# Attention values as the fixed operand of the value product, probabilities of two row blocks as the moving one

## The chip, the cores and the metric

The kernel runs on one core of a Trainium2 chip. The metric is the device time of one execution in microseconds; the median of three runs stands for a kernel. The engines are TensorE (PE, with its weight loads as PEld), VectorE (DVE), ScalarE (ACT), GpSimd (POOL) and SyncE (SP), which mostly starts transfers.

## The reference, cut to what matters

One step of a hybrid encoder layer on 1040 prompt rows (16 learned ones and 1024) and 32 sample rows with a cache of 512. Four mixers of 256 columns each; two of them are attention with 4 heads of 64. The prompt rows attend causally to the prompt rows.

```python
def fox_attend(q, k, v, f_q, f_k, q_pos, k_pos):          # mixer B, key "f" in the kernel
    s = jnp.einsum('bqhd,bkhd->bhqk', q, k).astype(jnp.float32) * (HEAD_DIM ** -0.5)
    s = s + (jnp.moveaxis(f_q, 2, 1)[..., :, None] - jnp.moveaxis(f_k, 2, 1)[..., None, :])
    s = jnp.where(k_pos[None, :] <= q_pos[:, None], s, -jnp.inf)
    p = jax.nn.softmax(s, axis=-1)
    return jnp.einsum('bhqk,bkhd->bqhd', p, v.astype(jnp.float32))

def sb_attend(q, k, v, q_pos, k_pos):                     # mixer C, key "s"
    z = jnp.einsum('bqhd,bkhd->bhqk', q, k).astype(jnp.float32) * (HEAD_DIM ** -0.5)
    mask = k_pos[None, :] < q_pos[:, None]
    log_keep = jnp.where(mask, jax.nn.log_sigmoid(-z), 0.0)
    later = lax.cumsum(log_keep, axis=3, reverse=True) - log_keep
    w = jnp.where(mask, jnp.exp(jax.nn.log_sigmoid(z) + later), 0.0)
    return jnp.einsum('bhqk,bkhd->bqhd', w, v.astype(jnp.float32))
...
    cat = jnp.concatenate([rms_norm(out_a, gains[0]), rms_norm(out_b..., gains[1]),
                           rms_norm(out_c..., gains[2]), o_d...], axis=-1)
    out = cat @ P['w_o'][l]
```

## The kernel before, in words

All products that matter for precision run in rounded parts: an operand x is written as hi (x rounded to fp32r) and lo (x - hi, rounded), and a product is hi*hi + lo*hi + hi*lo. ScalarE writes hi, GpSimd or VectorE writes lo. The exceptions are products in plain f32, the value product of attention among them.

The program is one long sequence: input norm and projections, the recurrent mixers, then `attention` (about 495 to 860 us of the span), then the FFN. Rows of the sequence are cut into 9 blocks `TB`: block 0 has 48 rows (32 sample rows, 16 learned ones), blocks 1 to 8 have 128. `attention` runs over key "s" (stick-breaking), then "f" (forgetting); in each over 4 heads, in each over the row blocks in the order `ROWS`, of which block 8 is cut into two chunks of keys: 10 positions a head, 40 a half. At each position t a software pipeline issues stage 0 of position t, stage 1 of t-1 and so on, in the order `ORDER`; `None` in it issues products of other work from the generators `fill` (projections of mixer f, output projections `w_o` of mixers a, d, s). That sets the priority of instructions; a planner of the framework orders them by priority as their operands and buffers come free.

Stages for "s": 0 scores on PE into two banks and a ScalarE copy; 1 `softplus_log`: min(z, 40) on VectorE, exp and ln on ScalarE; 2 `sb_sums`: max on VectorE, a running sum on VectorE, z minus the sum on GpSimd; 3 exp on ScalarE. For "f": 0 scores, bias and row maximum on VectorE; 1 exp on ScalarE. Then, for both, stage 4 `attn_turn`: PE transposes each 128x128 block of probabilities with the identity; VectorE copies the turned first 16 keys (L1338), VectorE or ScalarE copy the banks of four blocks to a tile `pt` (L1349, L142). Stage 5 `attn_row`: per row block one product per key block, the turned probabilities as the fixed operand, V (128 keys x 64 columns, for "f" 65 with a column of ones) as the moving one:

```python
self.mm(o, t0[:, :n], vm[:, h, :], True, j == 0)
for kb in range(1, j + 1):
    self.mm(o, pt[:, kb - 1, :], vt[(kb - 1) // 4][:, (kb - 1) % 4, h, :], False, kb == j)
```

The result has rows on partitions. VectorE writes it to `ot` (L1369), for "f" divided by the sum in column 64 (L1366, L176). `cat_rows` later turns `ot` on PE (L187) and copies it with the norm's gain to `cx` on ScalarE, splits it and multiplies with `w_o`; the rms comes from a ScalarE square with a row sum.

V comes from `proj_t_units`, which stores it to DRAM row by row; `load_v` reads it back in pieces of 64 columns. Score tiles are in slots of tag E, V and stacked queries and keys in slots U and T; `SLOTS` gives the numbers for U, E and X. `sample_attn` treats the 32 sample rows of all heads at once.

## Time and profile before

| | |
|---|---|
| median of 3 runs | 1669.48 us (1665.16 to 1672.03) |
| profiled execution | 1677.21 us, span 1675.5 us |
| mean granted clock of TensorE | 0.962 of full speed |
| PE busy | 1543.9 us (92%), 10536 instructions |
| PE weight loads | 1364.2 us (81%) |
| VectorE busy | 986.6 us (59%), 2008 |
| ScalarE busy | 681.3 us (41%), 1295 |
| GpSimd busy | 878.8 us (52%), 819 |

Shares of the whole span are averages over stages with different limits; the rows below are taken from the two halves of `attention`. In names of groups `out<-in1,in2` the first operand of a PE instruction is the moving one, the second the fixed one. A PE instruction's duration is a latency: neighbours overlap, and what one costs is the distance between starts.

### The profile page before, as it was taken

The page shows a single profiled execution, that of the slowest core. Times are in us where ns is not written, and L with a number is a line of the kernel's source. Part 1 is how long each engine was busy: PE and PEld are TensorE (multiplying, and loading weights), DVE is VectorE, ACT ScalarE, POOL GpSimd, SP SyncE. Part 2 cuts the span into 40 slices and gives each one's busy share as a digit, 9 for nine tenths or more (in the row PEclk, how much of TensorE's full clock was granted, in tenths as well). Part 3 has the DMA queues.
Part 4 walks back from the last instruction along what each step waited for, and adds up shares of the span by engine and source line. Part 5 has one row for each costly group of instructions (what it writes and reads, how often), then busy time and mean ns, then how long its engine had stood idle before and what let it go on. Part 6 is the DMA issues. An engine that isn't in the chain of part 4 may idle for free.

```text
span 1675.5 us, 27752 instructions
## 1 busy us (share of the span) xinstructions
PE 1543.9 (92%) x10536; PEld 1364.2 (81%) x10536; DVE 986.6 (59%) x2008; ACT 681.3 (41%) x1295; POOL 878.8 (52%) x819
## 2 busy tenths in 40 slices
PE   6988997799998999999987899999999999999997
PEld 4978986787778777778866899999999998878775
DVE  9835559844436688765687744444444443455466
ACT  4535424232234455544475333333333344333241
POOL 4563233342334335321028866776777769767575
PEclk9989999999999999999997899999999999999999
DMA  5152111312363742332030222222222247535460
GB/s 158 52 172 69 40 54 53 96 47 59 98 175 106 190 114 57 88 77 65 1 129 13 64 77 77 77 77 77 78 77 74 74 148 258 206 133 201 145 212 29
DMA packets 125934, 167.36 MB, mean 100 GB/s; under 512 B 23562, under 2 KB 102388, under 8 KB 125800
## 3 DMA queue, kind: packets, MB, share of 16 engines
q1 hardware_dynamic: 110969, 138.06, 26.8%
q10 hardware_dynamic: 14735, 27.51, 4.9%
q8 instruction: 83, 1.36, 0.4%
q14 instruction: 51, 0.42, 0.1%
q0 software_dynamic: 96, 0.01, 0.0%
HBM read 121.69 MB, written 43.86 MB: 99 GB/s over the span
## 4 chain that ended last, share of the span: by engine, by line
PE 38%; DVE 9%; POOL 6%; issue 4%; ACT 2%; DMA 1%; DVEq 0%; POOLq 0%; SPq 0%; ACTq 0%
PE ps L1877 14%; PE ps L183 11%; PE mm L183 6%; PE mm L1877 5%; DVE fy L180 3%; POOL wl L171 2%; PE ps L187 2%; PE pw L183 1%; POOL wlo L171 1%; POOL h L171 1%; DVE h L171 1%; DVE ws L171 1%; DMA wr<-in_ffn_w_in 1%; DVE fx L171 1%; POOL xl L171 1%
## 5 line engine op out<-in xcount | busy, mean ns | idle before, releaser
L1877 PE MATMUL ps<-xh,whi 128*128 128x256 f32 (+1 forms) x920 | 268.6, 292 | 20.4 <-DVE fu L171 11.5
L1877 PE MATMUL ps<-xl,whi 128*128 128x256 f32 (+1 forms) x920 | 266.3, 290 | 1.6 <-DVE xl L171 1.6
L1877 PE MATMUL ps<-xh,wlo 128*128 128x256 f32 (+1 forms) x920 | 266.0, 289 | 0.0
L1877 PEld LDWEIGHTS ps<-xh,whi 128*128 128x128 f32 x920 | 177.3, 193 | 24.8 <-DVE fu L171 14.0
L1877 PEld LDWEIGHTS ps<-xl,whi 128*128 128x128 f32 x920 | 177.5, 193 | 2.2 <-DVE xl L171 2.2
L1877 PEld LDWEIGHTS ps<-xh,wlo 128*128 128x128 f32 x920 | 177.2, 193 | 0.0
L171 POOL TENSOR_TENSOR wl<-wr,wh 128x1024 fp32r<-128x1024 f32 x58 | 147.4, 2551 | 31.8 <-ACT wh L142 30.5
L171 POOL TENSOR_TENSOR wlo<-ws,whi 128x512 fp32r<-128x512 f32 x92 | 127.6, 1388 | 36.1 <-ACT whi L142 27.9
L171 POOL TENSOR_TENSOR wlo<-wst,whi 128x512 fp32r<-128x512 f32 x54 | 73.6, 1368 | 91.0 <-ACT whi L142 73.5
L171 POOL TENSOR_TENSOR wlo<-wr,whi 128x512 fp32r<-128x512 f32 x69 | 92.6, 1342 | 37.7 <-ACT whi L142 37.7
L142 ACT ACTIVATE wh<-wr 128x1024 fp32r<-128x1024 f32 x58 | 60.7, 1057 | 125.0 <-POOL wl L171 110.1
L171 DVE TENSOR_TENSOR al<-ax,ah 128x768 fp32r<-128x768 f32 (+1 forms) x33 | 61.7, 1869 | 79.8 <-ACT ah L142 71.2
L142 ACT ACTIVATE whi<-ws 128x512 fp32r<-128x512 f32 x92 | 57.6, 626 | 122.8 <-PE ps L1877 53.6
L183 PE MATMUL ps<-wh,ah 128*128 128x512 f32 x264 | 104.8, 397 | 1.6 <-DVE h L171 1.6
L183 PE MATMUL ps<-wl,ah 128*128 128x512 f32 x264 | 104.6, 396 | 0.0
L183 PE MATMUL ps<-wh,al 128*128 128x512 f32 x264 | 104.5, 396 | 0.0
L180 DVE SCALAR_TENSOR_TENSOR fy<-fx,cf,fy 128x546 f32<-128x546 f32 (+1 forms) x88 | 97.1, 1119 | 11.2 <-ACT fy L143 9.4
L171 POOL TENSOR_TENSOR clo<-cx,chi 128x256 fp32r<-128x256 f32 (+1 forms) x36 | 27.6, 768 | 134.3 <-ACT chi L142 100.2
L1877 PE MATMUL mm<-xl,whi 128*128 128x274 f32 (+1 forms) x312 | 90.6, 290 | 4.7 <-DVE xl L171 2.5
L1877 PE MATMUL mm<-xh,whi 128*128 128x274 f32 (+1 forms) x312 | 90.6, 290 | 2.6 <-DVE fy L171 1.9
L1877 PE MATMUL mm<-xh,wlo 128*128 128x274 f32 (+1 forms) x312 | 90.3, 290 | 0.0
L183 PE MATMUL mm<-hh,whi 128*128 128x384 f32 (+1 forms) x240 | 85.8, 358 | 1.2 <-ACT ks L1209 1.2
(514 smaller groups left out, 4495.7 us busy)
## 6 DMA issues: line engine op xcount, KB each, us to landing
wr<-in_ffn_w_out SPq DMA_DIRECT2D x58, 512.0 KB
wr<-in_ffn_w_in SPq DMA_DIRECT2D x44, 512.0 KB
actd<-fy ACTq DMA_DIRECT2D x22, 529.0 KB
wst<-in_w_in SPq DMA_DIRECT2D x44, 256.0 KB
ax<-actd SPq DMA_DIRECT2D x22, 384.0 KB
x<-in_x_prompt SPq DMA_DIRECT2D x8, 512.0 KB
hd<-x SPq DMA_DIRECT2D x8, 512.0 KB
wst<-in_w_o SPq DMA_DIRECT2D x16, 256.0 KB
```

The source lines that it names most:

```text
L142: return self.nc.scalar.activation(out, in_, f, scale=scale, **k)
L171: return (eng or self.nc.vector).tensor_tensor(out, a, b, op)
L180: return (eng or self.nc.vector).scalar_tensor_tensor(out, a, s, b, op0, op1)
L183: return self.nc.tensor.matmul(out, l, r, start=start, stop=stop)
L187: return self.nc.tensor.transpose(out, in_, self.ident[:n, :n])
L1877: self.nc.tensor.matmul(ps, l[:, k], r[:, k], start=start and k + j == 0, stop=stop and k == 3 and j == 2, skip_group_check=not start)
```

## The change

V is split into hi and lo when it is projected and stored as two interleaved parts, so that a key block of a head is a fixed operand of 128 keys by 128 columns: 64 of hi beside 64 of lo. The probabilities of two neighbouring row blocks (1 and 2 with block 0, 3 and 4, 5 and 6, 7 and 8), turned, are the moving operand with up to 256 columns (272 with block 0), once their hi part and once their lo part. ScalarE writes hi from PSUM, VectorE lo. The result has features on partitions, the product with V's hi part in one half of them and with its lo part in the other; ScalarE copies the one and VectorE adds the other. `attn_pair` is a generator: a step of it issues one bank of transposes and the products of the bank before; `ORDER` has two steps ("p") per position.

The forgetting mixer takes the row sum from the exponential's accumulator and scales the probabilities by its reciprocal in a stage of its own (`fox_scale`). `softplus_log` computes ln(1 + exp(-|z|)) and adds max(z, 0) in `sb_sums`. The outputs need no turning before `w_o`; the norm's gain goes into the weights of `w_o`, and the sum of squares over features is a product with a column of ones (`rms_rows`). `fox_past`, a part of `fox_logf`, moves to just before the sample rows of the forgetting half. Slots: E 9 instead of 8, U 10 instead of 9, no X; three buffers each for the turned hi and lo parts. The order of row blocks changes.

```diff
             if key == "g":
+                nc.scalar.dma_start(dr[tb, :n], v[:n])
                 continue
+            vh, vl = self.H("vhi", 256, F32R), self.H("vlo", 256, F32R)
+            self.act(vh[:n], v[:n], AF.Copy)
+            self.tt(vl[:n], v[:n], vh[:n].bitcast(F32), OP.subtract, nc.gpsimd)
+            for t, o, step in ((vh, 0, 192), (vl, 64, 64)):
+                nc.scalar.dma_start(AP(dr, tb * P * 512 + o, [[512, n], [256, 2], [step, 2], [1, 64]]),
+                                    t[:n].bitcast(F32).rearrange("p (a e d) -> p a e d", a=2, e=2))
+            if tb == 0:
+                nc.scalar.dma_start(self.vs[key], v[:NS])
...
@@ -1276,22 +1292,20 @@
 
     def load_v(self, key):
 
-        nc = self.nc
-        vw = 65 if key == "f" else 64
...
+        v0 = self.U("v0", F32R, 768)
+        vm, vs = v0[:, 0:512], v0[:32, 512:768].bitcast(F32).rearrange("p (h d) -> p h d", h=4)
+        self.ts(vm, self.ones[:, 0:1].to_broadcast([P, 512]), 0.0, None, OP.mult)
+        vt = [self.U("v" + key, F32R, 1024, tag).rearrange("p (b h d) -> p b h d", b=2, h=4) for _ in range(4)]
+        dr = self.vd[key]
+        nc.sync.dma_start(vs.rearrange("p h d -> p (h d)"), self.vs[key])
+        nc.sync.dma_start(vm[:NM].bitcast(F32), dr[0, 32:48])
+        for i, t in enumerate(vt):
+            nc.sync.dma_start(t.bitcast(F32).rearrange("p b h d -> p b (h d)"),
+                              dr[1 + 2 * i:3 + 2 * i].rearrange("b p c -> p b c"))
+        return vs, vm.rearrange("p (h d) -> p h d", h=4), vt
...
+    def attn_pair(self, key, h, js, rows, done):
+        nc = self.nc
+        _, vm, vt = self.V[key]
+        pr, e = divmod(h, 2)
+        ja, jb = js
+        m = NM if ja == 1 else 0
+        w = 2 * P + m
+        o = None
+        def split(hi, lo, ps):
+            self.act(hi, ps, AF.Copy)
+            self.tt(lo, ps, hi.bitcast(F32), OP.subtract)
+        ps = self.PS()
+        c = 0
+        for j in ([0] if m else []) + [ja, jb]:
+            d = rows[key, h, j]
+            self.tr(ps[:16, c:c + d["n"]], d["blocks"][0])
+            c += d["n"]
+        th, tl = self.t0
+        split(th[:16, :w], tl[:16, :w], ps[:16, :w])
+        parts = [(vm[:, h], th[:, :w], tl[:, :w], 0)]
+        yield
+        for a in range(1, jb, 2):
+            late, parts = parts, []
             ps = self.PS()
+            c = 0
+            for kb in (a, a + 1):
+                c0 = c
+                for j in js:
+                    if kb <= j:
+                        self.tr(ps[:, c:c + P], rows[key, h, j]["blocks"][kb])
+                        c += P
+                parts.append((vt[(kb - 1) // 2][:, (kb - 1) % 2, h], c0, c, w - (c - c0)))
+            hi, lo = (self.up.tile([P, 512], F32R, name=self.nm(x), tag=x, bufs=NPT) for x in ("ph", "pl"))
+            split(hi[:, :c], lo[:, :c], ps[:, :c])
+            parts = [(v, hi[:, c0:c1], lo[:, c0:c1], at) for v, c0, c1, at in parts]
+            if o is None:
+                o = self.PS()
+            for v, x, y, at in late:
+                self.mm(o[:, at:w], v, x, a == 1, False)
+                self.mm(o[:, at:w], v, y, False, False)
+            yield
+        for i, (v, x, y, at) in enumerate(parts):
+            self.mm(o[:, at:w], v, x, False, False)
+            self.mm(o[:, at:w], v, y, False, i == len(parts) - 1)
+        own, other = slice(64 * e, 64 * e + 64), slice(64 - 64 * e, 128 - 64 * e)
+        o0, ot = self.ot[key]
+        u = ot[(ja - 1) // 4]
+        at = P * ((ja - 1) % 4)
+        for dst, src in (((o0[:, pr, 32:48], slice(0, m)),) if m else ()) + ((u[:, pr, at:at + 2 * P], slice(m, w)),):
+            self.act(dst[own], o[own, src], AF.Copy)
+            self.tt(dst[own], dst[own], o[other, src], OP.add)
+        for j in ([0] if m else []) + [ja, jb]:
+            del rows[key, h, j]
+            done(j)
...
-        stages = {"f": {0: self.fox_max, 1: self.fox_exp},
+        V, st, rows = self.V, self.stacks, {}
+        stages = {"f": {0: self.fox_max, 1: self.fox_exp, 2: self.fox_scale},
                   "s": {0: self.sb_scores, 1: self.sb_log, 2: self.sb_sum, 3: self.sb_exp}}
...
+        pairs, ready = deque(), {}
+        t = 0
+        def turned(key, h, j):
+            nonlocal fill, last
+            left = ready.setdefault((key, h), set(range(9)))
+            left.discard(j)
+            if key == "s" and h == 3 and not left:
+                for _ in fill:
+                    pass
+                fill = self.w_o_units("s")
+            if (key, h) == ("f", 3):
+                if last is None:
+                    last = self.w_o_units("f")
+                late.append((t + 1, j))
+        def step():
+            while pairs and next(pairs[0], "end") == "end":
+                pairs.popleft()
+        while t < len(runs) + 5 or pairs or late:
             if t == heads[1] - EARLY_A:
                 next(fill)
             if t == half - 8:
                 self.open_mixer("f")
             if t == half + 3:
-                self.sample_attn("f", V["f"][0], ot["f"][0], self.sample_load("f"))
+                self.fox_past()
+                self.sample_attn("f", V["f"][0], self.sample_load("f"))
...
+                if s == "p":
+                    step()
+                    continue
...
                 elif c[0] == 0 and s == 4:
-                    d["turned"] = self.attn_turn(key, j, d["blocks"], d["n"])
-                elif c[0] == 0 and s == 5:
...
+                    d["ready"] = True
+                    js = (j, j + 1) if j % 2 else (j - 1, j)
+                    if j and all(rows.get((key, h, i), {}).get("ready") for i in ((0, 1, 2) if j < 3 else js)):
+                        pairs.append(self.attn_pair(key, h, js, rows, lambda i, k=key, hh=h: turned(k, hh, i)))
...
-                i = ROWS.index(j)
+                i = WROWS.index(j)
...
-        self.act(p, p, AF.Exp, bias=d["mx"][:n, 2:3])
+        self.act(p, p, AF.Exp, bias=d["mx"][:n, 2:3], accum_out=d["mx"][:n, 3:4])
+        self.nc.vector.reciprocal(d["mx"][:n, 4:5], d["mx"][:n, 3:4])
+    def fox_scale(self, d, a, b, k0, k1):
+        if a:
+            return
+        n, j = d["n"], d["j"]
+        p = d["s"][:n, 0:16 + P * j]
+        self.act(p, p, AF.Copy, scale=d["mx"][:n, 4:5])
         d["blocks"] = self.row_blocks(0, j, p)
...
-        self.ts(e, z, 40.0, None, OP.min)
-        self.act(e, e, AF.Exp)
+        self.act(e, z, AF.Abs)
+        self.act(e, e, AF.Exp, scale=-1.0)
         self.act(e, e, AF.Ln, bias=1.0)
...
-        self.tt(e, z, e, OP.max)
+        self.stt(e, z, 0.0, e, OP.max, OP.add)
...
-        kc = self.E("kc", F32, 1024).rearrange("p (b d) -> p b d", b=4)
+        tag = "T" if key == "f" else "E"
+        kc = self.U("kc", F32, 1024, tag).rearrange("p (b d) -> p b d", b=4)
         nc.sync.dma_start(kc, I[kn].rearrange("a b (n p) h d -> p (a b n) (h d)", p=P))
...
+        vc = self.U("vc", F32, 1024, tag).rearrange("p (b h d) -> p b h d", b=4, h=4)
+        nc.sync.dma_start(vc.rearrange("p b h d -> p b (h d)"), I[vn].rearrange("a b (n p) h d -> p (a b n) (h d)", p=P))
...
+        gains = self.grp_g[:, 2 * {"f": 1, "s": 2}[mixer]:][:, 0:2] if mixer in "fs" else None
+        return [load(self.I["w_o"], P * k0, 2, 512 * half, 512, gains=gains) for half in range(2)]
...
+        if mixer in "fs":
+            x = self.ot_rows(mixer, tb)
+        else:
+            x = view("cx", F32)
...
-        else:
-            i = {"f": 1, "s": 2}[mixer]
-            ps = self.PS()
-            for pr in range(2):
-                self.tr(ps[:, P * pr:P * pr + n], ot[tb][:n, P * pr:P * pr + P])
-                self.act(x[:, pr], ps[:, P * pr:P * pr + n], AF.Copy, scale=self.grp_g[:, 2 * i + pr:2 * i + pr + 1])
+        hi, lo = view("chi", F32R), view("clo", F32R)
         self.act(hi, x, AF.Copy)
         self.tt(lo, x, hi.bitcast(F32), OP.subtract, self.nc.gpsimd)
         return [[a[:, k] for k in range(2)] for a in (hi, lo)]
...
+    def rms_rows(self, mixer, tbs, v, r, tm):
+        nc = self.nc
+        ps = self.PS()
+        for tb in tbs:
+            n = TB[tb][1]
+            sq = self.S1("sq").rearrange("p (a t) -> p a t", a=2)[:, :, :n]
+            self.act(sq, self.ot_rows(mixer, tb), AF.Square)
+            self.tt(sq[:, 0], sq[:, 0], sq[:, 1], OP.add, nc.gpsimd)
+            self.mm(ps[:n, tb:tb + 1], sq[:, 0], self.ones[:, 0:1], True, True)
+        a, c = tbs[0], slice(max(tbs[0], 1), tbs[-1] + 1)
+        if a == 0:
+            self.ts(v[:48, 0:1], ps[:48, 0:1], 1.0 / 256, RMS_EPS, OP.mult, OP.add)
+        self.ts(v[:, c], ps[:, c], 1.0 / 256, RMS_EPS, OP.mult, OP.add)
+        c = slice(a, tbs[-1] + 1)
+        self.rsqrt(r[:, c], v[:, c], tm[:, c])
...
             v, r = self.rms(i)
             tm = self.C([P, 9], f"rmst{i}")
+            if mixer == "s":
+                self.rms_rows(mixer, range(9), v, r, tm)
...
-            n, c = TB[tb][1], slice(tb, tb + 1)
-            x = self.cat_rows(mixer, tb, ot)
-            if ot is not None:
-                sq = self.S1("aosq")[:n]
-                self.act(sq, ot[tb][:n], AF.Square, accum_out=v[:n, c])
-                self.ts(v[:n, c], v[:n, c], 1.0 / 256, RMS_EPS, OP.mult, OP.add)
-                self.rsqrt(r[:n, c], v[:n, c], tm[:n, c])
-            return x
-
-        nx = rows(ROWS[0])
+            if mixer == "f":
+                for tbs in ((0, 1, 2), (3, 4), (5, 6), (7, 8)):
+                    if tb == next(j for j in WROWS if j in tbs):
+                        self.rms_rows(mixer, tbs, v, r, tm)
+            return self.cat_rows(mixer, tb)
...
-LATE_C = "mneg_r selh pt0".split()
-SLOTS = 9, 8, 2
+LATE_C = "mneg_r selh o0s o0f t0h t0l".split()
+SLOTS = 10, 9, 0
+NPT = 3
...
-ORDER = 0, 1, 3, 2, None, 5, 4
+ORDER = 0, 1, 3, 2, None, "p", 4, "p"
...
-ROWS = [0, 8, 1, 7, 2, 6, 5, 3, 4]
+ROWS = [0, 8, 7, 1, 2, 6, 5, 3, 4]
+WROWS = [7, 8, 0, 1, 2, 5, 6, 3, 4]
```

## Rows read from the trace of the kernel before

**Rows 1.** Windows: us; busy us of PE, PEld, DVE, ACT, POOL; clock; DMA

```profile
495.00:716.00 221.00, 201.21 (x1278) 166.30 (x1278) 170.57 (x363) 116.25 (x255) 87.34 (x76) 0.95 0.44 114
716.00:860.00 144.00, 142.44 (x907) 115.73 (x906) 93.96 (x359) 71.08 (x174) 19.86 (x23) 0.99 0.20 53
```

**Rows 2.** Chain of waits, shares by line: 716 to 868, then 560 to 716

```profile
by line: PE ps L183 32.5%; PE mm L183 30.4%; PE ps L187 16.3%; PE pw L183 13.3%; DVE h L180 2.2%; DVE bst L1746 1.6%; DVE bmv L171 1.0%; DVE h L171 0.9%; DVE rmst L180 0.8%; issue 0.7%; DVE bmv L176 0.2%; DVE rmst L171 0.2%; DVE rmst L177 0
...
by line: PE ps L183 4.7%; DVE sbe L1491 3.3%; PE mm L183 3.0%; PE pw L183 2.4%; ACT sbe L143 2.2%; DVE sbe L171 2.2%; POOL sbe L171 2.1%; DVE sb L176 1.9%; PE ps L187 1.5%; DVE sb L1491 1.3%; DVE h L171 1.3%; DVE pt L1349 1.1%; DVE sb L171 
```

**Rows 3.** Timeline of PE: start us, us, line, output<-moving,stationary, shapes, count

```profile
760.21 0.43 PE L183 MATMUL ps<-v,pt 16*128 16x65 f32 x2
760.57 2.00 PE L183 MATMUL ps<-vf,pt 128*128 128x65 f32 x16
762.41 0.38 PE L187 MATMUL ps<-ident,s 128*16 128x128 f32 x2
...
763.00 0.22 PE L183 MATMUL pw<-mneg_r,identr 128*128 128x128 f32 x1
763.06 0.28 PE L187 MATMUL ps<-ident,ot 128*128 128x128 f32 x1
```

**Rows 4.** Timeline of PE, first and last of 21 starts

```profile
527.45 0.28 PE L183 MATMUL mm<-wlo,hh 128*128 128x256 f32 x1
...
529.82 0.28 PE L183 MATMUL mm<-whi,hl 128*128 128x256 f32 x1
```

**Rows 5.** DVE by shape, 495 to 716: busy us, mean ns, idle before

```profile
L1257 DVE TENSOR_TENSOR_SCAN nfs<-ones,nfs 4x512 f32<-4x512 f32 x1 | 1.2, 1187 | 0.0
```

**Rows 6.** Groups by shape of ACT, 495 to 716

```profile
L142 ACT ACTIVATE pt<-ps 128x512 f32<-128x512 f32 x8 | 4.7, 589 | 2.4 <-PE ps L187 2.2
...
L142 ACT ACTIVATE pt<-ps 128x256 f32<-128x256 f32 x8 | 3.0, 376 | 6.5 <-PE ps L187 6.5
...
L142 ACT ACTIVATE pt<-ps 128x384 f32<-128x384 f32 x4 | 1.9, 474 | 0.7 <-PE ps L187 0.7
```

**Rows 7.** Groups by line of ACT, 495 to 716

```profile
L143 ACT ACTIVATE sbe<-sbe 128x896 f32<-128x896 f32 (+3 forms) x48 | 41.6, 874 | 33.9 <-POOL sbe L171 28.1 <-DVE sbe L176 5.8
L143 ACT ACTIVATE sb<-sb 128x144 f32<-128x144 f32 (+4 forms) x72 | 28.0, 405 | 18.8 <-POOL sb L171 14.1 <-DVE sb L176 4.4
...
L142 ACT ACTIVATE pt<-ps 128x512 f32<-128x512 f32 (+3 forms) x24 | 10.7, 447 | 16.1 <-PE ps L187 16.0
```

**Rows 8.** Groups by line of ACT, 716 to 862

```profile
L143 ACT ACTIVATE s<-s,mx 128x912 f32<-128x912 f32 (+8 forms) x33 | 24.4, 741 | 17.4 <-DVE mx L1472 17.4
L142 ACT ACTIVATE pt<-ps 128x512 f32<-128x512 f32 (+3 forms) x32 | 16.5, 517 | 41.8 <-PE ps L187 41.7
L142 ACT ACTIVATE cx<-ps,cf 128x128 f32<-128x128 f32 (+1 forms) x34 | 12.1, 355 | 11.7 <-PE ps L187 11.4
...
L143 ACT ACTIVATION_READ_ACCUMULATOR aosq<-ot 128x1 f32 x9 | 1.8, 195 | 0.0
```

**Rows 9.** Groups by line of DVE, 495 to 716

```profile
L176 DVE TENSOR_SCALAR sb<-sb 128x144 f32<-128x144 f32 (+4 forms) x24 | 14.0, 583 | 4.9 <-ACT sb L142 4.8
L1349 DVE COPY pt<-ps 128x512 f32<-128x512 f32 (+2 forms) x24 | 13.9, 581 | 1.9 <-PE ps L187 1.9
L176 DVE TENSOR_SCALAR sbe<-sbz 128x896 f32<-128x896 f32 (+3 forms) x16 | 13.5, 846 | 1.4 <-ACT sbz L142 1.4
...
L171 DVE TENSOR_TENSOR h<-h,mm 128x512 f32<-128x512 f32 (+1 forms) x17 | 11.3, 667 | 1.4 <-PE mm L183 1.3
L1338 DVE COPY pt<-ps 16x128 f32<-16x128 f32 (+1 forms) x36 | 9.2, 255 | 3.0 <-PE ps L187 2.8
L1369 DVE COPY ot<-ps 128x64 f32<-128x64 f32 x32 | 6.8, 211 | 8.5 <-PE ps L183 8.3
```

**Rows 10.** Windows of 20 us with a lower clock, columns as in rows 1

```profile
580.00:600.00 20.00, 17.73 (x100) 14.56 (x99) 19.81 (x34) 9.76 (x19) 7.40 (x7) 0.84 0.38 102
...
880.00:900.00 20.00, 13.64 (x68) 11.78 (x69) 14.52 (x14) 11.74 (x19) 20.00 (x11) 0.67 0.00 1
```

185 lines of the change are left out of this document (65 added, 120 removed).

## Prediction

> **What bounds the kernel now.** The windows by stage come first, because the change stays inside two of them. Values are multiplied from about 495 to 860 us: the stick-breaking half to 716, the forgetting half after it. In [rows 1] the second column is TensorE's busy time. In the forgetting half it is 142.4 of 144 us at a granted clock of 0.99, with VectorE at 94 and ScalarE at 71. The chain of waits agrees: from 716 to 868 us its shares by line are nearly all PE, 32.5% at L183 into `ps` (the value products) and 16.3% at L187 (transposes) [rows 2]. That half is bound by TensorE, and time taken from PE there comes back almost whole. The stick-breaking half is mixed: PE 201, VectorE 171, ScalarE 116, GpSimd 87 of 221 us, and its chain runs through all four [rows 1, 2]. There a saving on one engine comes back in part.
>
> **What a value product costs now.** In the timeline, `x16` of the value products start at 760.57 and the next instruction at 762.41 [rows 3]: 16 records in 1.84 us, 0.115 each. Each key block is two records, so 0.230 us per block and row block. The 16-key product takes from 760.21 to 760.57, 0.36 us. A head has 36 blocks and 8 full 16-key products (row block 0 left out): 36 x 0.230 + 8 x 0.36 = 11.2 us.
>
> **What it costs afterwards.** A product in rounded parts with 256 moving columns has a row: from 527.45 to 529.82 lie 20 gaps, so 0.119 each [rows 4]; with 128 columns one starts at 763.00 and the next instruction at 763.06, 0.06 [rows 3]. Over the pairs (1,2), (3,4), (5,6), (7,8) a head has 2+4+6+8 = 20 products that serve both row blocks (the first also serves row block 0, with 272 columns) and 4 that serve one, each for the high and the low part: 40 x 0.119 + 8 x 0.06 = 5.2 us. So 6.0 us of PE go per head, 24 per half, 48 in all. The transposes of the probabilities keep their number.
>
> The Trainium skill, "FP8 and Floating Point Precision", TensorE Precision Notes, counts a true FP32 product as four passes through the array. By that an old block of 65 columns would stream 260 columns, 0.108 us by estimate at the higher clock, and the new block 2 x 128, the same: nothing would be saved on PE. The trace has two records and 0.230 us per block, so the rule is a rival with a small chance (below).
>
> **Other PE work.** Turning the outputs before the output projection goes: 36 transposes over both mixers, 128 columns and a weight load each like the records of [rows 3], 0.115 by those, so 4. The sums of squares come as 18 products with one column, two records each: 36 x 0.115 = 4 back (bounds: nothing, if they slip between, and 36 x 0.36/2 = 6.5). These cancel. But each new product waits for a ScalarE square and a GpSimd addition and stands in PE's order. For the stick-breaking mixer all nine come in a row at the change of halves: nine times a square like the 0.4 us pass in [rows 6] is 4 us of possible stall, and four groups in the forgetting half are like it, 1 us each. The cover is w_o and score products already queued; if it fails, 8 us. I take 4. `fox_past` moves from the fifth row block of the first w_o product to just before the sample rows of the forgetting half: one small SP load behind those of the cached keys and values, four transposes, three VectorE operations (a scan of 512 takes 1.2 [rows 5]) and two GpSimd selects. On PE the sample scores and all that stands behind them would wait. I take 0, since the first forgetting scores are queued ahead; uncovered it is the two scans and the minus pass, about 3, beside the load. The cached tiles move to T slots, free once the last odd head's scores are done: 0 for the same reason.
>
> **ScalarE takes over what PE and VectorE give up.** Stick-breaking: a pass for |z| comes, as large as one of the three passes in (41.6 + 28.0)/3 = 23 us [rows 7]. Splitting comes: per head 6 banks of 512 at 0.589, 4 of 384 at 0.474 and 4 first parts at the 0.376 of 256 columns [rows 6]: 6.9 us, 28 per half. The old copies (10.7) go [rows 7]. Output copies come, 4 per head at 0.376: 6. Net about +46: 116 becomes 162. Forgetting: a pass that scales the probabilities comes, as large as the exponentials (24.4 for 33, so 26 for 36 [rows 8]); reading 36 row sums, 0.19 by the sum read after the squares [rows 8], 7; splits 28; output copies 6; squares of the other mixer 4 and eight gains on weights at about 0.6, 5. The old copies (16.5) and the turned outputs (12.1) go [rows 8]. Net +47, some 5 of it hidden because neighbouring passes overlap: 71 becomes about 113.
>
> **VectorE.** Stick-breaking gives up the minimum (13.5 + 14.0), copies (13.9 + 9.2) and output copies (6.8): 57 us [rows 9]. It takes the low parts: 24 banks at the 0.667 of a pass with a PSUM operand over 512 columns, 16 of 384 (0.55, scaled from the same row), 16 small ones at 0.4: 31; output additions 7. Net -19: 171 becomes 152. The maximum that becomes a maximum and an addition keeps its size: nothing. The forgetting half gets about 10 more, beside 94: hidden.
>
> The Trainium skill, "ScalarE: Activation LUTs", Rules for kernel authors, gives minima, additions and multiplications to VectorE and not to ScalarE, against two moves of this change. Here the rows don't show VectorE ahead: 40 minima took 27.5 us [rows 9], one ScalarE pass of the same size 23 [rows 7]. By the rule VectorE would return less and ScalarE would bind sooner, which is the third case.
>
> **The sum.** Forgetting half: PE 144 - 24 + 4 = 124, above ScalarE's 113; with two engines this close I add 4 for hand-overs (a pair runs PE, ScalarE, VectorE, PE): 128, so -16. Stick-breaking half: engines at 177, 162 and 152 where they were 201, 116 and 171. If PE alone sets its length, which was 1.10 times PE's busy time, 177 gives 195, -26. If the chain through VectorE and ScalarE sets it, VectorE's -19 is half eaten by the extra ScalarE passes in the same chain, -10. No row decides between them; I take the middle, -18. The end: row blocks 3 and 4 now end together, after one more stage and up to three pair steps, so one more row's evacuation and statistics stand after the last value product: +2 (bounds 0, if the queued w_o products cover it, and 6). V is written in more, smaller pieces and read in longer ones, under the projections, with 18 extra ScalarE copies there: 0 (cover: dense PE work; without it 18 x 0.4 = 7, and -2 if the longer reads help). Together -16 - 18 + 2 = -32. The profiled execution took 1677.2 us around its span of 1675.5, 7.7 above the median of 1669.5; -32 gives 1645 against it and **1637** beside the median.
>
> **Rivals.**
> First: everything comes back. PE's 48 us, plus the waits that VectorE's 19 causes in the first half (its chain shows VectorE lines [rows 2]), -50 to -60: 1610 to 1620. For it: PE fills the forgetting half. Against it: ScalarE's 113 is only 11 behind.
> Second: ScalarE and the clock take most of it. ScalarE's queue is in order, and the splits feed PE, so each pass ahead of a split is a PE wait; and when PE waits its clock falls: 0.84 between 580 and 600 us with PE busy 17.7 of 20, 0.67 between 880 and 900 with 13.6 [rows 10]. If the first half ran at 0.84 instead of its 0.95, its 177 us of PE become 200 and nothing is left there; -16 and +2 remain, with up to 8 of stalls against them or a third of the first half's -18 kept: -6 to -20, 1650 to 1663.
> Third, slower: the buffers. A row's score tile was free after stage 4; now it lives until its pair is turned. By the order of rows and two pair steps a position, some 10 tiles (and in the forgetting half two bias tiles) want 9 E slots around position 8 of each head, so the scores of the last two row blocks wait for pair (7,8). A position is 221/40 = 5.5 us in the first half, 144/40 = 3.6 in the second; two lost positions a head are 4 x 11 + 4 x 7.2 = 73 us, and 73 - 48 + 2 = +27: 1696. It decides from a loss of 6 us a head, about one position in the first half. Against it: PE has w_o products to fill with, and the average demand fits.
> Fourth: the change doesn't do what it says: the saving on PE isn't there (four passes in the old product, or the new ones stream slower than [rows 4]): ScalarE's additions then cost what they can't hide, 1668 to 1676.
>
> **How the numbers follow.** Forecast 1637 (1625 to 1648) 0.46; first rival 0.16; second 0.24, of which 0.04 lies within 0.5%; third 0.10, most of it slower, a little of it (0.02) within; fourth 0.04, within or slower. A measurement tells about 0.5% (8 us) from no change, so faster is below 1661: 0.46 + 0.16 + 0.20 = 0.82; same 0.08; slower 0.10. The range, 1611 to 1667, leaves out the slower cases and the far end of the first.
>
> **What would show it.** Value products of 256 columns starting about 0.12 us apart, a forgetting half of about 128 us still led by PE with ScalarE near 110, a stick-breaking half near 203. Wrong if scores wait for score tiles, if PE's largest wait in either half is a ScalarE split, or if the clock in the first half falls below 0.9.

## The result, and the profile after

The kernel after takes 1692.95 us (median of 6 runs, 1680.14 to 1694.85) against 1670.46 for the kernel before (6 runs): ratio 1.0127, 95% interval 1.0084 to 1.0169. It is slower by some 22 us; forecast were 32 us less. Its profiled execution took 1694.13 us around a span of 1692.4, 16.9 more than the span before.

Where do they lie? The stages of the two programs stand at different times, so fixed windows compare different work. The cuts below are made at the same events: the first score of the stick-breaking half (PE, `pw<-kst,qst` of row block 0), of its second head, of the forgetting half, and the first FFN product. Windows of before, columns as in [rows 1]:

```profile
0.00:491.60 491.60, 434.83 (x3386) 386.31 (x3387) 295.59 (x701) 187.17 (x394) 192.58 (x246) 0.96 0.29 86
491.60:553.60 62.00, 56.45 (x420) 50.67 (x418) 37.86 (x69) 27.80 (x54) 24.87 (x19) 0.96 0.53 151
553.60:685.00 131.40, 119.96 (x678) 96.43 (x677) 110.75 (x212) 73.84 (x156) 57.14 (x51) 0.92 0.41 105
685.00:879.70 194.70, 183.66 (x1170) 148.19 (x1168) 132.97 (x498) 100.19 (x249) 32.04 (x36) 0.98 0.26 72
879.70:1675.50 795.80, 749.04 (x4889) 682.64 (x4889) 409.41 (x530) 292.31 (x445) 572.15 (x469) 0.97 0.33 110
```

The same five of after, and the two fixed windows of [rows 1] again:

```profile
0.00:497.00 497.00, 442.09 (x3378) 393.58 (x3379) 295.96 (x703) 190.88 (x404) 199.17 (x255) 0.94 0.30 89
497.00:567.60 70.60, 54.66 (x376) 48.89 (x373) 30.89 (x44) 35.53 (x73) 29.18 (x27) 0.93 0.46 128
567.60:711.50 143.90, 114.51 (x576) 89.37 (x577) 113.64 (x176) 101.48 (x222) 55.66 (x47) 0.86 0.40 111
711.50:898.10 186.60, 166.85 (x984) 136.17 (x982) 139.97 (x424) 136.08 (x310) 40.16 (x53) 0.93 0.27 78
898.10:1692.40 794.30, 749.36 (x4889) 682.84 (x4889) 409.97 (x530) 293.28 (x446) 571.49 (x470) 0.97 0.33 111
...
495.00:716.00 221.00, 171.35 (x962) 139.85 (x962) 149.27 (x226) 140.51 (x300) 86.42 (x75) 0.88 0.43 120
716.00:860.00 144.00, 136.44 (x830) 113.04 (x831) 101.41 (x293) 109.37 (x253) 29.98 (x41) 0.92 0.23 58
```

To the first score +5.4, first stick-breaking head +8.6, the three others +12.5, forgetting half -8.1, the rest -1.5. Read the third row of both: TensorE has 5 us less to do and the stage is 12.5 longer; VectorE, which was to give up work, has 3 us more; ScalarE 28 more; the granted clock fell from 0.92 to 0.86. No engine is full. The last two rows mislead: 149 for VectorE between 495 and 716 is close to the forecast's 152, but the window of before had 31 us of the forgetting half in it, that of after less than 5.

TensorE's own change is as forecast. PE's timeline of after, high and low parts with 256 columns 0.12 us apart, with 128 columns 0.06, against [rows 3, 4]:

```profile
779.56 0.28 PE L184 MATMUL ps<-ph,vf 128*128 128x256 f32 x1
779.68 0.28 PE L184 MATMUL ps<-pl,vf 128*128 128x256 f32 x1
...
780.26 0.22 PE L184 MATMUL ps<-ph,vf 128*128 128x128 f32 x1
780.32 0.27 PE L184 MATMUL ps<-pl,vf 128*128 128x128 f32 x1
```

VectorE, 495 to 716: groups of after that answer to [rows 9] (busy us, mean ns, idle before):

```profile
L172 DVE TENSOR_TENSOR pl<-ps,ph 128x512 fp32r<-128x512 f32 (+1 forms) x33 | 20.2, 631 | 7.6 <-ACT ph L143 7.6
L181 DVE SCALAR_TENSOR_TENSOR sbe<-sbz,sbe 128x896 f32<-128x896 f32 (+3 forms) x16 | 18.8, 1178 | 9.5 <-ACT sbe L144 9.3
L181 DVE SCALAR_TENSOR_TENSOR sb<-sb 128x144 f32<-128x144 f32 (+4 forms) x23 | 17.3, 751 | 13.0 <-ACT sb L144 12.9
...
L172 DVE TENSOR_TENSOR t0l<-ps,t0h 16x256 fp32r<-16x256 f32 (+1 forms) x13 | 5.4, 412 | 4.4 <-PE ps L184 2.3 <-ACT t0h L143 2.0
L172 DVE TENSOR_TENSOR ot<-ot,ps 64x256 f32<-64x256 f32 x12 | 5.1, 421 | 0.8 <-ACT ot L143 0.4
```

Before, the plain maximum stood where lines 2 and 3 are (groups of before, same window):

```profile
L171 DVE TENSOR_TENSOR sbe<-sbz,sbe 128x896 f32<-128x896 f32 (+3 forms) x16 | 18.8, 1176 | 8.4 <-ACT sbe L143 8.4
L171 DVE TENSOR_TENSOR sb<-sb 128x144 f32<-128x144 f32 (+4 forms) x24 | 12.1, 507 | 3.5 <-ACT sb L143 3.4
```

The mean on the narrow tiles rose from 507 ns to 751, on the wide ones it stayed. The means mix shapes and hide what happened, so here are single instructions on 128x656, first of before, then of after:

```profile
595.95 0.83 DVE L171 TENSOR_TENSOR sbe<-sbz,sbe 128x656 f32<-128x656 f32 x1
638.88 2.02 POOL L171 TENSOR_TENSOR sbe<-sbz,sbe 128x784 f32<-128x784 f32 x1
639.07 2.53 DVE L171 TENSOR_TENSOR sbe<-sbz,sbe 128x656 f32<-128x656 f32 x1
...
616.10 0.83 DVE L181 SCALAR_TENSOR_TENSOR sbe<-sbz,sbe 128x656 f32<-128x656 f32 x1
710.50 1.87 POOL L172 TENSOR_TENSOR sbe<-sbz,sbe 128x784 f32<-128x784 f32 x1 [7.61 <-DVE sbc L177]
710.84 2.23 DVE L181 SCALAR_TENSOR_TENSOR sbe<-sbz,sbe 128x656 f32<-128x656 f32 x1
```

The maximum with an addition takes as long as the plain one, 0.83 us, and each is more than twice as long where it runs at the same time as a GpSimd instruction. Over the four heads 13 of the 38 maxima of after are more than 0.15 us above the shortest of their shape, 6 of 38 before, by 11.2 and 4.9 us in all. Every one of these overlaps a GpSimd instruction (182 of 182 over the twenty kernels of this document); others overlap one and stay short, so an overlap doesn't always cost. The rise is thus not the price of the new instruction.

ScalarE's groups of after, for [rows 7]: one pass more over `sb` and `sbe`, and the splits:

```profile
L144 ACT ACTIVATE sb<-sb 128x144 f32<-128x144 f32 (+4 forms) x92 | 33.4, 396 | 10.6 <-POOL sb L172 6.1 <-POOL vlo L172 4.2 <-ACT sb L143 0.2
L143 ACT ACTIVATE ph<-ps 128x512 fp32r<-128x512 f32 (+1 forms) x34 | 17.6, 543 | 0.0
L144 ACT ACTIVATE sbe<-sbz 128x896 f32<-128x896 f32 (+3 forms) x16 | 14.0, 876 | 11.1 <-POOL sbe L172 10.6 <-PE ps L188 0.5
...
L143 ACT ACTIVATE vhi<-vst 128x256 fp32r<-128x256 f32 (+1 forms) x9 | 3.7, 412 | 10.0 <-POOL sb L172 6.0 <-DVE vst L172 3.9
```

What PE waits for in the three later stick-breaking heads (us, times, longest), after, then before:

```profile
PE mm L184 <- DVE sbc L177: 6.8, 2, 3.4
PE mm L184 <- POOL clo L172: 4.4, 5, 2.4
PE mm L184 <- ACT chi L143: 4.0, 2, 2.4
PE ps L188 <- ACT sbe L144: 3.4, 1, 3.4
PE ps L184 <- ACT t0h L143: 2.1, 2, 1.3
```

```profile
PE ps L183 <- DVE pt L1338: 2.2, 4, 1.1
PE mm L183 <- DVE h L180: 2.0, 1, 2.0
PE pw L183 <- ACT sb L142: 1.7, 2, 1.5
```

The largest is not a split of the probabilities: w_o products (`mm`) wait for a bank that VectorE has to empty. Of its two waits, the one that ends at 698.50 has VectorE in its stick-breaking chain (two running sums stand ahead of the addition that empties the bank); in the one that ends at 574.60 VectorE itself had waited 3.1 us for the load `h<-hd`, a wait that the same stretch of before doesn't have.

### The profile page after: what moved, and what is told of

Its sections match the earlier page's. It is cut to its first block, busy times and chain, and to the rows that moved or that the text cites. A ratio compares the mean times of both kernels' runs of the same rounds, so it can differ in the third digit from the quotient of the medians.

```text
span 1692.4 us, 27179 instructions
## 1 busy us (share of the span) xinstructions
PE 1527.5 (90%) x10200; PEld 1350.9 (80%) x10200; DVE 990.4 (59%) x1876; ACT 757.3 (45%) x1452; POOL 895.7 (53%) x850
## 4 chain that ended last, share of the span: by engine, by line
PE 28%; POOL 10%; DVE 8%; issue 5%; ACT 4%; DMA 3%; SPq 0%; POOLq 0%; DVEq 0%; ACTq 0%
PE ps L1949 14%; PE mm L1949 6%; POOL wl L172 4%; PE ps L184 4%; PE mm L184 3%; POOL wlo L172 2%; DVE fy L181 2%; POOL h L172 2%; DMA wr<-in_ffn_w_in 2%; DVE h L172 1%; DMA wr<-in_ffn_w_out 1%; PE pw L184 1%; PE ps L188 1%; DVE h L181 1%; POOL xl L172 1%
## 5 line engine op out<-in xcount | busy, mean ns | idle before, releaser
L143 ACT ACTIVATE wh<-wr 128x1024 fp32r<-128x1024 f32 x58 | 60.7, 1056 | 125.3 <-POOL wl L172 111.2
L172 POOL TENSOR_TENSOR wlo<-wst,whi 128x512 fp32r<-128x512 f32 x56 | 77.5, 1388 | 70.1 <-ACT whi L143 55.7
L181 DVE SCALAR_TENSOR_TENSOR fy<-fx,cf,fy 128x546 f32<-128x546 f32 (+1 forms) x88 | 97.1, 1119 | 11.2 <-ACT fy L144 9.4
L184 PE MATMUL mm<-hh,wlo 128*128 128x384 f32 (+1 forms) x240 | 82.4, 344 | 1.4 <-POOL wlo L172 1.4
```

What stands on the lines that cost most here:

```text
L143: return self.nc.scalar.activation(out, in_, f, scale=scale, **k)
L172: return (eng or self.nc.vector).tensor_tensor(out, a, b, op)
L181: return (eng or self.nc.vector).scalar_tensor_tensor(out, a, s, b, op0, op1)
L184: return self.nc.tensor.matmul(out, l, r, start=start, stop=stop)
```

## The experiments

Theory at the outset: the splits on ScalarE and the V storage sit in ScalarE's in-order queue among passes that wait, and PE waits behind them. Rivals: score buffers (the slower rival of the prediction), V storage by itself, VectorE's queue. The ratios of the experiments are against the kernel before, run beside them in five rounds (medians 1671.9 to 1672.7). That of after is the one of the result, six runs against six, and has the widest interval of all; a gain against after is a difference of two such ratios, shown where the intervals lie apart. Stage times are those of one profile each; the stage after the first FFN product, which no edit touches, ranges over them from 789.7 to 799.6, so a single stage tells nothing below some 5 us.

| kernel | ratio, 95% | first score | first s head | s heads 2-4 | f half |
|---|---|---|---|---|---|
| before | 1 | 491.6 | 62.0 | 131.4 | 194.7 |
| after | 1.0127 (1.0084-1.0169) | 497.0 | 70.6 | 143.9 | 186.6 |
| b_vsplit | 1.0055 (1.0037-1.0072) | 490.7 | 71.4 | 128.5 | 193.2 |
| a_vraw | 1.0044 (1.0026-1.0061) | 492.0 | 65.6 | 141.9 | 184.8 |
| a_vfix | 1.0062 (1.0039-1.0085) | 486.3 | 74.4 | 135.8 | 185.6 |
| a_vload | 1.0092 (1.0064-1.0120) | 489.8 | 75.2 | 142.7 | 182.7 |
| a_vload_sp | 1.0093 (1.0057-1.0128) | 495.4 | 75.5 | 144.9 | 183.2 |
| b_softplus | 0.9987 (0.9967-1.0007) | 494.2 | 61.4 | 135.3 | 190.9 |
| a_softplus | 1.0069 (1.0045-1.0093) | 494.3 | 67.6 | 143.0 | 180.4 |
| a_ord | 1.0092 (1.0070-1.0115) | 491.5 | 68.0 | 144.5 | 184.6 |
| a_p3 | 1.0091 (1.0068-1.0114) | 499.0 | 70.0 | 146.5 | 184.4 |
| a_hidve | 1.0081 (1.0058-1.0104) | 492.2 | 69.7 | 141.7 | 184.7 |
| a_nolo | 1.0045 (1.0025-1.0064) | 498.3 | 70.3 | 133.8 | 187.4 |
| a_e10 | 1.0043 (1.0023-1.0063) | 493.9 | 68.6 | 144.0 | 178.9 |
| a_npt2 | 1.0108 (1.0081-1.0136) | 491.0 | 69.4 | 144.4 | 185.6 |
| a_e10_vfix | 1.0036 (1.0018-1.0054) | 491.0 | 73.3 | 135.7 | 179.0 |
| a_three | 0.9917 (0.9891-0.9943) | 488.3 | 64.1 | 129.3 | 181.6 |
| hybrid | 1.0085 (1.0059-1.0111) | 492.4 | 75.6 | 128.2 | 197.1 |
| hybrid2 | 0.9964 (0.9941-0.9986) | 489.4 | 67.1 | 136.9 | 175.7 |
| hybrid3 | 0.9992 (0.9976-1.0009) | 490.1 | 67.5 | 134.3 | 183.6 |

### V storage

**b_vsplit**: the storing alone, put into the kernel before (the cut lines store both parts to a table of their own).

```diff
             nc.scalar.dma_start(dr[tb, :n], v[:n])
+            vh, vl = self.H("vhi", 256, F32R), self.H("vlo", 256, F32R)
+            self.act(vh[:n], v[:n], AF.Copy)
+            self.tt(vl[:n], v[:n], vh[:n].bitcast(F32), OP.subtract, nc.gpsimd)
...
```

> The kernel before, with the value splitting of the kernel after added (ScalarE copy, GpSimd subtraction, two stores into a table of their own that nothing reads). Theory (value storage costs ScalarE-queue and tile waits under the projections and the first head): +8 to +14 us, 1680 to 1686. Rival (it costs only where the paired attention stands beside it): 0 to +3, 1672 to 1675.

9 us by the ratio. In the profile the first head takes 9.4 more (62.0 to 71.4), where mixer f's values are projected beside attention, but that execution was as a whole no longer than the one of before (spans 1675.4 and 1675.5), and its second head is 2.1 shorter. From kernel to kernel the first two heads trade time, so they are better read as one: 100.7 us before, 107.9 here. The largest waits in the first head that name the new tiles:

```profile
DVE vst L171 <- POOL vlo L171: 5.5, 1, 5.5
ACT sbz L142 <- POOL vlo L171: 4.7, 1, 4.7
```

A score copy on ScalarE stands behind a wait for GpSimd's low part.

**a_vraw**: the splitting left out of the kernel after, which stores V itself in both places and so leaves its low part out; the stores stay.

```diff
-            vh, vl = self.H("vhi", 256, F32R), self.H("vlo", 256, F32R)
-            self.act(vh[:n], v[:n], AF.Copy)
-            self.tt(vl[:n], v[:n], vh[:n].bitcast(F32), OP.subtract, nc.gpsimd)
+            vh = vl = v
```

> The kernel after without splitting the values where they are stored: the raw values are written in both places, so no ScalarE copy, no GpSimd subtraction and no extra tiles there (the low part of the values is wrong for it). Rival (value storage costs the 5 us before the first score and much of the 9 us of the first head): 1678 to 1685. Theory (ScalarE's queue under attention): 1688 to 1693.

14 us come back, with intervals apart, and the first two heads take 111.2 us instead of 118.2. From both sides V storage is worth 9 to 14 us by the ratios, and 7 of them are seen in the first two heads.

**a_vfix**: the same pieces by VectorE, stored by SyncE.

```diff
-            self.act(vh[:n], v[:n], AF.Copy)
-            self.tt(vl[:n], v[:n], vh[:n].bitcast(F32), OP.subtract, nc.gpsimd)
+            nc.vector.tensor_copy(vh[:n], v[:n])
+            self.tt(vl[:n], v[:n], vh[:n].bitcast(F32), OP.subtract)
...
-                nc.scalar.dma_start(AP(dr, tb * P * 512 + o, [[512, n], [256, 2], [step, 2], [1, 64]]),
+                nc.sync.dma_start(AP(dr, tb * P * 512 + o, [[512, n], [256, 2], [step, 2], [1, 64]]),
```

> The kernel after with the value splitting on VectorE alone (high part and low part) and its stores issued by SyncE instead of ScalarE, so that no attention pass on ScalarE stands behind a wait for GpSimd's low part. Theory (the cost of value storage is the wait in ScalarE's queue): most of the 13 us that leaving the splitting out gave, 1681 to 1685. Rival (it is the tiles and the transfers, which stay): 1690 to 1695.

11 us back by the ratios (the intervals just meet), with the work and the transfers still there. That fits a cost which lies in the place, ScalarE's and GpSimd's queues, but the profile doesn't show the place: heads 2 to 4 fall to 135.8, but the first rises to 74.4, so that the first two together take 115.5, 2.7 less than in after; and 10.7 of the difference stand before the first score, where the two profiles of this edit differ by 5 us (486.3 here, 491.0 in a_e10_vfix). The run also moves splitting and stores at once.

**a_vload, a_vload_sp**: V stored raw and split once in `load_v`, in the second with the softplus of before.

```diff
+            self.act(hi, st[:, :, e::2], AF.Copy)
+            self.tt(lo, st[:, :, e::2], hi.bitcast(F32), OP.subtract, nc.gpsimd)
```

> The kernel after with the values stored raw as before, and split once when a mixer's values are loaded (per mixer 10 ScalarE copies and 10 GpSimd subtractions of up to 256 columns, into the tiles that hold the values) instead of 9 times per mixer between projection and store. Theory (storing in pieces costs 9 to 14 us by waits in ScalarE's queue and tiles under the first head): 1679 to 1684. If the work itself, not the place, costs: 1690 to 1695.

> a_vload with the softplus of before as well. If the gains of the two (-10 to -14, -10) add up: 1668 to 1674. If they are the same waits: 1678 to 1684.

Two misses: 6 us back by the medians, with intervals that overlap that of after, and the softplus adds nothing to it. The first head stays at 75 us, so by these profiles the new place is no better.

### Softplus, order of steps, who copies

**b_softplus, a_softplus**: the softplus edit alone on before, and undone on after.

```diff
-        self.ts(e, z, 40.0, None, OP.min)
-        self.act(e, e, AF.Exp)
+        self.act(e, z, AF.Abs)
+        self.act(e, e, AF.Exp, scale=-1.0)
...
-        self.tt(e, z, e, OP.max)
+        self.stt(e, z, 0.0, e, OP.max, OP.add)
```

> The kernel before with the softplus of after alone (absolute value on ScalarE, maximum and addition in one VectorE instruction, no minimum): VectorE 27 us less, ScalarE 23 more in the stick-breaking half. If VectorE leads that half's chain: -5 to -10, 1662 to 1667. If the chain as a whole sets it, the passes being as long on either engine: within 4 us of 1672. If ScalarE's queue is what costs: +5 to +10, 1677 to 1682.

> The kernel after, with the softplus of before in the stick-breaking half (a minimum on VectorE and a plain maximum, no absolute value on ScalarE): ScalarE 23 us less there, VectorE some 27 more. Theory (ScalarE's queue): the stick-breaking heads shrink by 5 to 10 us, 1683 to 1688. If VectorE is as much in that chain as ScalarE: 1690 to 1700. Buffers or value storage: no change, 1693.

On before the edit is worth nothing. On after, undoing it gives some 10 us (the intervals just overlap), but not in the stick-breaking heads 2 to 4 (143.0), so the forecast place was wrong. In its profile 6 of them lie in the forgetting half (180.4 against 186.6), almost all in its first head (48.4 against 54.3), which begins at the change of halves.

**a_ord, a_p3, a_hidve**: a pair step moved ahead of the exponential; a third pair step per position; the high part in "s" copied by VectorE.

```diff
-ORDER = 0, 1, 3, 2, None, "p", 4, "p"
+ORDER = 0, "p", 1, 3, 2, None, 4, "p"          # a_ord
+ORDER = 0, 1, 3, 2, "p", None, "p", 4, "p"     # a_p3
...
-            self.act(hi, ps, AF.Copy)
+            self.nc.vector.tensor_copy(hi, ps)   # a_hidve, key "s" only
```

> The kernel after with one of the two pair steps of a position moved up, ahead of the position's logarithm, exponential and sum stages, so that its splits don't stand behind an exponential that waits for GpSimd. Theory (ScalarE's queue): TensorE's waits for splits fall and 5 to 10 us come back, 1683 to 1688. Rivals (buffers, value storage): within 3 us of 1693. If the score copies and logarithms behind the splits matter more: slower, 1695 to 1705.

> The kernel after with three pair steps a position instead of two. A head needs 18 steps and has 20, so a pair that is ready late pushes the later ones into the next head, and their rows' score buffers stay taken. If that backlog costs (buffers, drain): 1680 to 1687. If ScalarE's or VectorE's queue sets the pace whatever the place of the steps: 1689 to 1696.

> The kernel after with the high part of the probabilities in the stick-breaking half copied by VectorE, directly ahead of its low part, instead of by ScalarE: ScalarE 28 us less there, VectorE as much more, and one hand-over between engines less in each split. Theory (TensorE waits there for splits that stand in ScalarE's queue): 5 to 10 us come back, 1682 to 1688. Rival (VectorE's queue is as bad, with w_o additions behind it): 1690 to 1700.

Each gives 6 to 8 us by its median, with intervals that overlap that of after: none of the three gains is shown. And none shortens heads 2 to 4 by more than a profile's uncertainty (144.5, 146.5, 141.7). ScalarE's queue alone is not what holds these heads: that part of the theory falls.

### VectorE's low parts

**a_nolo**: in "s" the low part of the probabilities is left out.

```diff
-            self.tt(lo, ps, hi.bitcast(F32), OP.subtract)
+            if key == "f":
+                self.tt(lo, ps, hi.bitcast(F32), OP.subtract)
...
-                self.mm(o[:, at:w], v, y, False, False)
+                if key == "f":
+                    self.mm(o[:, at:w], v, y, False, False)
```

> The kernel after without the low part of the probabilities in the stick-breaking half: no subtraction on VectorE (some 31 us less there) and no second product on TensorE (some 10 less); it leaves that part of the result out. If VectorE's queue sets the three later heads (143 us against 131): they fall by 10 or more, 1676 to 1684. If ScalarE's queue does (splits' high parts, absolute values): 1688 to 1693.

14 us back, and here heads 2 to 4 do fall, from 144 to 133.8. Their window, to be read against the third row of after above:

```profile
568.60:702.40 133.80, 102.71 (x510) 79.19 (x510) 94.59 (x134) 97.77 (x217) 52.86 (x47) 0.87 0.42 115
```

VectorE is 19 us lower, ScalarE 4, PE 12. PE's largest waits in that window, to be read against those of after above:

```profile
PE mm L184 <- ACT chi L143: 14.0, 6, 3.5
PE mm L184 <- POOL clo L172: 10.4, 7, 5.1
```

The waits for VectorE's bank, 6.8 us in after, are down to 1.8, and those for w_o's parts have grown from 8.4 to 24.4. So I read the gain as VectorE's queue, with ScalarE and GpSimd next in line; but the run relieves VectorE and PE together and doesn't separate them.

### Score buffers

**a_e10** and its control **a_npt2**: ten E slots instead of nine, paid for with one pair of split tiles; the control pays without getting the slot.

```diff
-SLOTS = 10, 9, 0
-NPT = 3
+SLOTS = 10, 10, 0      # a_e10; unchanged in a_npt2
+NPT = 2                # both
```

> The kernel after with ten score buffers instead of nine, and two pairs of split tiles instead of three to make room for it. Rival of the prediction (rows wait for score buffers until their pair is turned): the three later stick-breaking heads, 144 us against 131 before, give back 5 to 10 us, 1683 to 1688. If buffers don't matter: 1690 to 1697 (the third pair of split tiles gone may cost a little).

> The kernel after with two pairs of split tiles instead of three and nine score buffers as before: the control for the run with ten buffers, which had both edits and was 14 us below the kernel after. If the tenth buffer gave that: 1690 to 1697 here. If the order that comes out of fewer split tiles gave it: 1678 to 1684.

1.0043 against 1.0108, intervals apart: the tenth buffer is worth 11 us. They don't lie where I expected them, in heads 2 to 4, but as far as the profiles show them in the forgetting half: 178.9 against 185.6 (179.0 and 181.6 in the two later kernels with ten), 16 us below before, the forecast's -16. That is 6.7 of the 11; the two profiled executions as a whole differ by 1.6 only. At the change of halves one sees how. Windows of 5 us of after, then of a_e10 at the same events:

```profile
711.00:716.00 5.00, 1.40 (x6) 0.67 (x5) 4.96 (x6) 2.63 (x5) 2.07 (x2) 0.85 0.59 200
716.00:721.00 5.00, 4.52 (x15) 3.69 (x16) 3.75 (x8) 3.39 (x8) 3.08 (x3) 0.50 0.27 71
...
751.00:756.00 5.00, 3.75 (x27) 3.27 (x25) 1.31 (x7) 3.50 (x11) 2.62 (x6) 0.95 0.56 158
756.00:761.00 5.00, 4.60 (x16) 4.17 (x17) 3.69 (x10) 5.00 (x10) 0.44 (x1) 0.50 0.00 2
```

```profile
706.00:711.00 5.00, 4.38 (x25) 3.11 (x23) 4.91 (x7) 5.00 (x10) 1.15 (x1) 1.00 0.09 26
711.00:716.00 5.00, 3.67 (x21) 3.01 (x21) 4.94 (x10) 2.80 (x7) 4.73 (x4) 1.00 0.43 108
716.00:721.00 5.00, 4.27 (x29) 3.73 (x29) 3.52 (x12) 4.10 (x13) 3.80 (x5) 1.00 0.02 5
```

In both VectorE is full with the last stick-breaking rows. With nine buffers PE has 1.4 of 5 us of work meanwhile, and then runs at half the clock (0.50 is the lower level, 1.2 GHz); with ten it has 4.4 and 3.7 and keeps the higher one. In after a second fall follows at 756. What PE waits for between 711 and 717, in after:

```profile
713.80 0.38 PE L184 MATMUL ps<-ph,vs 128*128 128x256 f32 x1 [1.79 <-ACT ph L143]
716.41 0.58 PE L184 MATMUL ps<-pl,vs 128*128 128x256 f32 x1 [2.23 <-DVE pl L172]
```

These are waits for the split parts of the last stick-breaking rows, the low one behind VectorE's maximum of 2.23 us shown above and the running sum after it. The control a_npt2 has the same two waits, 1.79 and 2.23. With ten buffers PE has w_o products between them and waits 0.2 for `pl`. No wait in the trace names a score tile; that it is the buffer is shown by the runs, not by a row.

### Together, and without pairs in the first half

**a_e10_vfix** has the two edits above with the whole result computed; **a_three** has a_e10, a_vraw and a_nolo in one (the parts left out are theirs).

> The kernel after with the tenth score buffer (two pairs of split tiles) and the value splitting on VectorE with stores by SyncE, the whole result computed. Singly these gave -14 and -11 us. If they are two causes in two places (first head; change of halves): they add, 1666 to 1672, level with the kernel before. If they take away the same waits: 1677 to 1682.

> The kernel after with three suspected costs taken away at once: the tenth score buffer, no splitting of the values where they are stored (raw values in both places), and no low part of the probabilities in the stick-breaking half (the last two leave parts of the result out). Singly -14, -13 and -12. If these three are the whole difference between the forecast and the measurement and add up: 1650 to 1658. If they overlap: 1664 to 1675, and the forecast's gain in the stick-breaking half isn't there even without them.

The first two don't add: 0.0091 of the 0.0149 that they gave singly. All three give 0.0210 of 0.0249, and the kernel is then 0.8% faster than before. So they overlap in part, and take away more than the loss against before. That is an upper bound, since a_three leaves out work that the forecast had counted. They are not the whole difference from the forecast: even so the stick-breaking heads 2 to 4 stand at 129.3 against 131.4, so the forecast's gain there isn't found.

**hybrid**: "s" as before (products, V, turning, statistics), "f" in pairs. **hybrid2**: V of "f" split in `load_v`, `SLOTS = 9, 9, 3` instead of `8, 9, 2` (the split tiles in the third X slot). **hybrid3**: a tenth E slot and the old `ROWS` in "s".

```diff
+                elif c[0] == 0 and s == 4 and key == "s":
+                    d["turned"] = self.attn_turn(key, j, d["blocks"], d["n"])
+                elif c[0] == 0 and s == 5 and key == "s":
+                    self.attn_row(key, h, j, d["turned"], d["n"], V[key], self.ot[key])
```

> The stick-breaking half does its value products, value storage, output turning and row statistics as in the kernel before; only the forgetting half uses pairs of row blocks and rounded parts (softplus stays as in the kernel after). Theory (ScalarE's queue in the stick-breaking half: splits stand behind passes that wait): the stick-breaking heads go back from 214 to about 195-200 us, the middle forgetting heads keep 27 us: 1655 to 1667. Rival (storing values in pieces under the projections): half of that storing stays, 1670 to 1680. Rival (score buffers): would also give 1660 to 1670, so it is not told apart here.

> Only the forgetting half with pairs and rounded parts; the stick-breaking half as before, values of the forgetting mixer split when they are loaded, and one more slot for the tiles for which the change of halves waited 12 us in the first hybrid. Theory (pairs cost some 12 us in the three later stick-breaking heads and give 10 to 16 in the forgetting half, the value storage 9): stick-breaking heads as before, forgetting half -10 to -14, 1656 to 1663. If the pairs are not what slows the stick-breaking heads: 1668 to 1680.

> The second hybrid (pairs in the forgetting half alone, values split when loaded) with ten score buffers and the old order of row blocks in the stick-breaking half. If buffers and order add to it: 1655 to 1662, faster than both kernels. If they were only worth something under the pairs of the first half: 1664 to 1669.

The first was a miss: heads 2 to 4 are back at 128.2, but eight U slots held up the first forgetting head (64 us, 54 in after), whose queries and keys wait for them: SyncE's load of the last of them stood 14.9 us behind PE. With the slot given, hybrid2 beats both kernels: 0.9964, about 6 us. Its two attention stages from the second head on:

```profile
556.50:693.40 136.90, 120.67 (x672) 97.55 (x673) 99.64 (x183) 87.18 (x186) 63.62 (x57) 0.87 0.43 102
693.40:869.10 175.70, 162.68 (x1007) 130.99 (x1005) 138.74 (x462) 136.03 (x341) 35.67 (x44) 0.99 0.28 81
```

The forgetting half is 19 below before, at a clock of 0.99. The first head keeps 5 us and the next three 5 of loss, which stay unexplained (the softplus of after is still in); hybrid3's edits don't mend them (0.9992). Its tenth buffer doesn't help the forgetting half either (183.6): without pairs in the first half nine are enough.

## Why the prediction was wrong, step by step

In the profiles the forecast of -32 and the measured +16.9 lie 49 us apart. 39 of them are in the stick-breaking half (-18 forecast, 21.1 longer), 6 in the forgetting half with its tail (-14 forecast, 8.1 shorter), 5 ahead of the first score.

- **Value products** (-6.0 us a head): right. In the forgetting half the middle heads went from 32.9 and 33.4 to 26.9 and 26.9. The four-pass rival falls with that.
- **Forgetting half, -16**: the size holds with a tenth buffer (-15.8); as built it is -8.1, lost to the change of halves. The forecast took PE as its bound. The four PE lines that made 92.5% of the chain of waits from 716 to 868 in [rows 2] make 48.6% of it in after, and VectorE and ScalarE stand between them, which the added 4 us of hand-overs allowed for in part. That -15.8 meets -16 is partly luck: the last head, up to the first FFN product, gave nothing (76.7 before, 78.5 after, 77.2 with ten buffers), where -6 and +2 of tail were forecast, and with ten buffers the first gave 6.5, at the change of halves.
- **V storage, 0 (bounds +7, -2)**: the step that failed most plainly. Dense PE work was named as its cover. It covers mixer s (in b_vsplit the first score comes at 490.7, before at 491.6), but mixer f is projected under the first stick-breaking head, where ScalarE's queue serves attention; 9 to 14 us by the ratios.
- **Stick-breaking half, -18**: this is where the sign was lost. Of the middle between "PE sets its length" and "the chain does", the first was wrong: its products fell and nothing came of it. VectorE's -19 was mis-sized. Its busy time over the four heads fell from 148.6 to 144.5, and over heads 2 to 4 it rose by 3. The rows it was summed from, 495 to 716, reached into the forgetting half. The low parts and output additions came back as forecast, 31 by then. What failed is the saving: of the 25.9 us of minima in the four heads of before, 10.9 lie above the shortest record of each shape, nearly all of it in 16 records that each overlap a GpSimd instruction. By that an estimated 15 us were the minimum's own. "Keeps its size: nothing" was right for the instruction, but the maxima overlapped GpSimd more often and took 6 us more. With VectorE little lighter and ScalarE 35 heavier in a chain through all four engines, the stage grew; that the one follows from the other is argued, not shown. a_nolo shows that the low parts, on VectorE and PE together, are worth 14 us. The Trainium skill ("ScalarE: Activation LUTs", Rules for kernel authors) keeps minima, additions and multiplications off ScalarE; that move cost nothing on before, and undoing it on after gave some 10 us by medians whose intervals just overlap, so at most the rule holds here where ScalarE has the splits as well.
- **ScalarE and the clock (second rival)**: its sign was seen (clock in the first half below 0.9: 0.86 in heads 2 to 4, 0.92 before), but PE's largest waits there were VectorE's bank and w_o's parts, not splits of the probabilities. For those it waited at the change of halves, 1.79 and 2.23 us, and there the clock fell to 0.50.
- **Score buffers (third rival)**: a buffer is worth something, as it said, and its side was right, but not its place and price: 11 us, seen at the change of halves, instead of two positions lost in every head, 73. No wait for a score tile was seen. It had 0.10, and that its 1696 lies near the measured 1693 is luck. What the range lacked was that several small losses, each with a bound of its own in the text, would come together: +9 to 14 for V, 11 for buffers, and no gain in the first half.
- **Open**: whether moving a step, adding one and moving a copy give anything; why undoing the softplus helps at the change of halves; where a_vfix's gain lies; how a_nolo's gain divides between VectorE and PE; the 10 us that hybrid2's first half still loses.

## What to carry to other kernels

Cut two traces at the same events before comparing busy times; a fixed window counts the neighbour's work as a saving. In a stage whose chain runs through four engines, none of them full, a saving on one comes back only if the next in the chain doesn't get heavier, and work that is "hidden" must be placed in the queue it will stand in, not in the stage it belongs to. A busy time can hold time spent beside another engine: before counting an instruction as a saving, compare its mean with the shortest record of its shape. When tiles live longer, price the buffer at the seam between stages too, where PE runs dry and the clock falls.
